# State-space products in rings of their own: what more temporary tiles do to a scheduled kernel

## The chip, the core and the metric

The kernel runs on one core of one Trainium2 chip. The metric is the device time of one execution in microseconds (us). On the core, TensorE (PE) multiplies matrices, VectorE (DVE), ScalarE (ACT) and GpSimd (POOL) work element by element, and SyncE (SP) issues the transfers of the DMA engines. Each engine takes its own instructions strictly in the order in which they stand in its queue. They wait for each other by semaphores.

## The reference

One layer of an encoder over 1024 positions of width 1024, all in float32:

```python
xn = rmsnorm(h, g_mix); proj = xn @ w_in
u, v = proj[..., :512], proj[..., 512:]
y_ssm = s5_mixer(u, ...)                    # 32 groups of 16 channels, 64 complex states, two directions
y_fft = fourier_mixer(v, w_fourier)         # 4 heads: real part of a 2-d FFT, then a 128x128 product
h = h + concatenate([y_ssm, y_fft]) @ w_out
h = h + conv_ffn(rmsnorm(h, g_ffn), w_up, conv_w, conv_b, w_down)   # 1024 -> 2x2816 -> 1024, width-3 convolution
return rmsnorm(h, g_final)

# s5_direction, run once per direction
lam_bar = exp(lam * dt)
b_bar = ((lam_bar - 1.0) / lam)[..., None] * b
bu = einsum('gph,blgh->blgp', b_bar, uf)
_, states = associative_scan(_ssm_combine, (a, bu), reverse=reverse, axis=1)
return einsum('ghp,blgp->blgh', c, states).real
# s5_mixer: y = both directions + d_skip * uf;  z = gelu(y);  z * sigmoid(z @ w_glu + b_glu)
```

## The kernel before

The sequence is cut into 128 chunks of 8 positions. Within a chunk the state-space part is a product with small matrices, and only the state at the chunk borders runs through a scan. The 32 groups are worked in 16 batches of two groups, b = 0 to 15. Four batches share a column tile `ct` of 128 channels, so batches 12 to 15 belong to tile 3. For each batch the program writes these steps, each a function:

- `prep(b)` (P): input factors. For the real and the imaginary part a product `b` of 128x512 (L666) and a sum of its halves into `bt` (L667). PE transposes `bt` (`pbm`) and multiplies it for the Toeplitz kernel (`pk`, L130). After every fourth batch `toeplitz` follows, with some DMAs through `dd`, `kd` and `tm`.
- `tables(b)` (T): twiddle tables `wt`. Two products `w` of 128x256 (L710), two sums (L712), two copies on ACT (L714).
- `out_matrix(b)` (OM): output factors `cm`. Two products `c` of 128x512 (L721), a sum (L723) and a difference (L725).
- `inputs(b)` (I): the matmuls `ps`, inputs to the states.
- `states(b)` (S): two products `r` of 128x512 from the incoming states in PSUM and `wt` (L745), sums into `scd` (L747, L749), four scans into `so` (L756, L757), two products `x` of 128x512 from the outgoing states and `wt` (L763), and two sums into `yy` (L764).
- `outputs(b)` (O): the matmuls `py` with `tm`, `yy` and `cm`, and after every fourth batch `gelu_out`: transposes `pyt` and a Gelu into `z`. `zsplit(ct)` splits `z` into high and low parts in `zf`.

Around these stand the products with `w_in` (`pin`), the Fourier part of four heads (splits `fw` and `yf`, evictions `yfs`, matmuls `pq`, `pe`, `po`), and the lower half of `w_out` (tokens WL and WB): `w_out_load(n)` loads and splits the four blocks k of column half n (`wo`, L155, one split each on DVE or POOL), and `w_out_bottom(n, s)` makes the 12 matmuls `pwo` of token tile s. DVE adds each result to `h` (L931). Behind the state-space part follow the gate products `pg` (weights `wg`, input `zf`), the upper half of `w_out`, a norm, the up projection as seven block products (`u`) with the convolution and gate, the down projection (`dqa`, `dqb`), and the final norm.

A float32 product of full precision is made of three matmuls of split operands, high and low.

Two things set the order of the work. The order in which the program is written is a string of tokens for this part, `SEQ`, and a table `OPT` says for each product and sum whether DVE or POOL does it. The change touches neither. The order in which instructions stand in each engine's queue is then set by the framework's scheduler, which plans with costs of its own and knows which tile each instruction writes. A tile comes from a ring: `bufs` tiles of one tag, handed out in turn. An instruction that takes a ring's next tile cannot run until the last reader of that tile's earlier content has run, so the size of a ring decides both waits and the plan.

Before, the rings of this part are: `t2`, two tiles of 2 KB per partition, shared by the products `b`, `r` and `x`; and `t3`, one tile, shared by `w`, `c` and the temporary `tw` of `phase_tables` (L511), where POOL makes the phase tables.

Of the kernel before, what the change touches and what calls it, by code (L numbers as in the profile page):

```python
# [20 lines left out]
P = 128  # L21
# [60 lines left out]
def bc(ap, axis, n):  # L82
    ap = ap.unsqueeze(axis)
    shape = list(ap.shape)
    shape[axis] = n
    return ap.broadcast_to(shape)
# [3 lines left out]
def encoder_block(  # L90
# [8 lines left out]
    V, A, PE, GP = nc.vector, nc.scalar, nc.tensor, nc.gpsimd  # L99
# [9 lines left out]
    def opt(key, default):  # L109
        v = OPT.get(key, default)  # L110
        return {"V": V, "G": GP}.get(v, v) if isinstance(v, str) else v
# [137 lines left out]
    def q(name, shape=(P, G), dt=F32, tag="q", bufs=13):  # L249
        return sp.tile(list(shape), dt, name=name, tag=tag, bufs=bufs)  # L250
# [4 lines left out]
    NG = 2  # L255
    NB = G // NG
# [77 lines left out]
    pwr, pwi, ta, tb = (pw[:, i] for i in range(4))  # L334
# [5 lines left out]
    def pair(a):  # L340
        return a.rearrange("p (b g) -> p b g", g=NG)
# [40 lines left out]
    def cmul(eng, outr, outi, ar, ai, br_, bi_, ta, tb):  # L382

        eng.tensor_mul(ta, ar, br_)
        eng.tensor_mul(tb, ai, bi_)
        eng.tensor_sub(outr, ta, tb)
        eng.tensor_mul(ta, ar, bi_)
        eng.tensor_mul(tb, ai, br_)
        eng.tensor_add(outi, ta, tb)

    def csq(c, s_, name):

        a, b, c2, s2 = (q(f"{name}_{k}") for k in "abcs")
        V.tensor_sub(a, c, s_)
        V.tensor_add(b, c, s_)
        V.scalar_tensor_tensor(s2, c, 2.0, s_, ALU.mult, ALU.mult)
        V.tensor_mul(c2, a, b)
        return c2, s2
# [96 lines left out]
    def phase_tables(lv):  # L495
        wt_ = w1t if lv == 4 else w2t
        te = opt(f"ph{lv}", GP)
        if lv == 4:
            ec, es, ecn = (prv[k] for k in ("ec", "es", "ecn"))
            esd = q("esd")  # L500
            V.tensor_copy(esd[0:64], es[0:64])
            V.tensor_copy(esd[64:128], ecn[64:128])
            prv["cur"] = (ec, esd)
        cur = prv["cur"]
        wr, wi = wt_[:, :, 0], wt_[:, :, 1]
        if lv == 2:
            GP.memset(wr[:, :, :, 0], 1.0)
            GP.memset(wi[:, :, :, 0], 0.0)
        for j in range(lv):
            n = 1 << j  # L510
            tw = q(f"tw{lv}_{j}", (P, 2, NB, NG, 8), tag="t3" if te is GP else "t2", bufs=1 if te is GP else 2)  # L511
            cmul(te, wr[:, :, :, n:2 * n], wi[:, :, :, n:2 * n], wr[:, :, :, :n], wi[:, :, :, :n],
                 bc(pair(cur[0]), 3, n), bc(pair(cur[1]), 3, n), tw[:, 0, :, :, :n], tw[:, 1, :, :, :n])
            cur = csq(cur[0], cur[1], f"wq{lv}_{j}")
        prv["cur"] = cur
        if lv == 2:
            GP.tensor_copy(w2t[:, :, 2], w2t[:, :, 0])
# [119 lines left out]
    def t2(name):  # L637
        return q(name, (P, 2 * NG * P), tag="t2", bufs=2)

    def prep_ct(ct):  # L640

        for dst, i in ((cbr, 0), (cbi, 1)):
            for d in range(2):
                hs = slice(64 * d, 64 * d + 64)
                A.activation(
                    dst[hs, :, d].rearrange("p (b g) h -> p b g h", g=NG),
                    rawc[hs, 4 * ct:4 * ct + 4, i], AF.Copy)
        cts[ct].kf = q(f"kf{ct}", (P, 8, 16), tag="kf", bufs=1)
        cts[ct].kb = q(f"kb{ct}", (P, 8, 16), tag="kb", bufs=1)
# [8 lines left out]
    def prep(b):  # L658

        c, ct, sb = bs[b], b // 4, b % 4  # L660
        if sb == 0:
            prep_ct(ct)
        bt = q(f"bt{b}", (P, 2, NG, 8, 16), tag="bt", bufs=1)
        for i, op in ((0, ALU.subtract), (1, ALU.add)):
            m = t2(f"b{b}_{i}").rearrange("p (n s h) -> p n s h", n=2 * NG, s=8)
            opt(f"pb{b}{i}", V).tensor_mul(m, slots(gst, b, i), heads(rawb, b))  # L666
            opt(f"pa{b}{i}", V).tensor_tensor(bt[:, i], m[:, 0:NG], m[:, NG:2 * NG], op)  # L667
        c.bm = q(f"bm{b}", (P, 2, NG, P), tag="bm", bufs=NBM)
        pt = bank2(f"pbm{b}")
        btv = bt.rearrange("p i g s h -> p (i g) (s h)")  # L670
        for n in range(2 * NG):
            PE.transpose(pt[:, n * P:(n + 1) * P], btv[:, n], ident)
        A.activation(c.bm.rearrange("p i g n -> p (i g n)"), pt, AF.Copy)
        pk = bank2(f"pk{b}")
        for g in range(NG):
            for i, cc in ((0, cbr), (1, cbi)):
                mm(pk[:, g * 32:(g + 1) * 32], btv[:, i * NG + g],
                   cc[:, NG * sb + g].rearrange("p d h -> p (d h)"), start=(i == 0), stop=(i == 1), key=f"pk{b}")
        pkv = pk[:, :NG * 32].rearrange("p (g d h) -> p g d h", g=NG, d=2)
        A.activation(cts[ct].kf[:, NG * sb:NG * sb + NG], pkv[:, :, 0], AF.Copy)  # L680
        A.activation(cts[ct].kb[:, NG * sb:NG * sb + NG], pkv[:, :, 1], AF.Copy)
        if sb == 3:
            toeplitz(ct)
# [20 lines left out]
    def tables(b):  # L704

        c = bs[b]
        c.wt = q(f"wt{b}", (P, 2, NG, 8, 16), tag="wt", bufs=2)
        for i, op in ((0, ALU.subtract), (1, ALU.add)):
            m = q(f"w{b}_{i}", (P, 2 * NG, 4, 16), tag="t3", bufs=1)
            opt(f"tw{b}{i}", GP).tensor_mul(m, bc(w1t[:, b].rearrange("p i g n -> p (i g) n"), 2, 4),  # L710
                                            bc(w2t[:, b, i:i + 2].rearrange("p i g n -> p (i g) n"), 3, 16))
            opt(f"ta{b}{i}", GP).tensor_tensor(c.wt[:, i, :, 4:8], m[:, 0:NG], m[:, NG:2 * NG], op)  # L712
            wf = c.wt[:, i].rearrange("p g j n -> p g (j n)")
            A.activation(wf[:, :, 0:64], wf[:, :, 127:63:-1], AF.Copy, scale=(-1.0 if i else 1.0))  # L714

    def out_matrix(b):
        c = bs[b]
        c.cm = q(f"cm{b}", (P, 2, NG, 8, 16), tag="cm", bufs=3)
        for i in range(2):
            m = q(f"c{b}_{i}", (P, 2 * NG, 8, 16), tag="t3", bufs=1)  # L720
            opt(f"tc{b}{i}", GP).tensor_mul(m, slots(pst, b, i), heads(rawc, b))  # L721
            if i == 0:
                opt(f"td{b}{i}", GP).tensor_add(c.cm[:, 0], m[:, 0:NG], m[:, NG:2 * NG])  # L723
            else:
                opt(f"td{b}{i}", GP).tensor_sub(c.cm[:, 1], m[:, NG:2 * NG], m[:, 0:NG])  # L725
# [10 lines left out]
    def states(b):  # L736

        c = bs[b]
        pst_ = c.ps
        A.activation(scr[:, :, 1:129], bc(r8[:, NG * b:NG * b + NG], 2, NCH), AF.Copy)  # L740
        sv = pst_.rearrange("p (i g c) -> p i g c", i=2, g=NG)
        wv = c.wt.rearrange("p i g j n -> p i g (j n)")
        for i in range(2):
            m = t2(f"r{b}_{i}").rearrange("p (i g c) -> p i g c", i=2, g=NG)
            V.tensor_mul(m, sv, wv if i == 0 else wv[:, ::-1])  # L745
            if i == 0:
                opt(f"ra{b}{i}", V).tensor_add(scd[:, 0, :, 1:129], m[:, 0], m[:, 1])  # L747
            else:
                opt(f"ra{b}{i}", V).tensor_sub(scd[:, 1, :, 1:129], m[:, 1], m[:, 0])  # L749
        n = 2 * NG * W  # L750
        so = q(f"so{b}", (P, 2 + n), tag="so", bufs=1)
        m = NG * W
        rf = scr.rearrange("p g w -> p (g w)")
        for i in range(2):
            df = scd[:, i].rearrange("p g w -> p (g w)")
            V.tensor_tensor_scan(so[0:64, 2 + i * m:2 + i * m + m], rf[0:64], df[0:64], 0.0, ALU.mult, ALU.add)  # L756
            V.tensor_tensor_scan(so[64:128, i * m:i * m + m][:, ::-1], rf[64:128, ::-1], df[64:128, ::-1], 0.0,  # L757
                                 ALU.mult, ALU.add)
        xs = so[:, 2:2 + n].rearrange("p (i g w) -> p i g w", i=2, g=NG)[:, :, :, :NCH]
        c.yy = q(f"yy{b}", (P, 2, NG, NCH), tag="yy", bufs=2)  # L760
        for i, op in ((0, ALU.subtract), (1, ALU.add)):
            m = t2(f"x{b}_{i}").rearrange("p (i g c) -> p i g c", i=2, g=NG)
            opt(f"xm{b}{i}", V).tensor_mul(m, xs, wv if i == 0 else wv[:, ::-1])  # L763
            opt(f"xa{b}{i}", V).tensor_tensor(c.yy[:, i], m[:, 0], m[:, 1], op)  # L764

# [627 lines left out]
    for i in range(2):  # L1393
        w = outer.tile([P, 2, 512], F32R, name=f"du{i}", tag="wp", bufs=NWP).bitcast(F32)
# [69 lines left out]
```

## Time and profile before

| | us |
|---|---|
| median of 3 runs | 1059.65 (1057.95 to 1060.36) |
| the profiled execution | 1058.18 |
| its span, first to last instruction | 1056.4 |
| PE busy in the span | 970.4 (92%) |
| DVE busy | 937.7 (89%) |
| ACT busy | 466.0 (44%) |
| POOL busy | 232.1 (22%) |

All times of the prediction come from the one profiled execution. Roughly, the span begins with norm and pole tables (to about 84 us), goes on with the state-space and Fourier parts (to about 306), the rest of the lower `w_out` and the gate (to about 359), the upper `w_out` and a norm (to about 440), the up projection (to 780) and the down projection with the final norm. Rows of stretches give for each engine the busy time and, in brackets, the number of instructions; then the share of TensorE's clock that was granted, the busy share of the DMA engines, and GB/s. Rows of waits read "engine, result, line, <- what released it: us in total, times, longest". Rows of a timeline read "start, duration, what"; in brackets the idle time just before and its releaser.

### The profile page before, as it was taken

To read this page: it belongs to the slowest core of one execution; us is meant where nothing else is said; L and a number is where in the kernel's file an instruction comes from. 1 tells how busy PE (TensorE), PEld (TensorE's weight loads), DVE (VectorE), ACT (ScalarE), POOL (GpSimd) and SP (SyncE) were. 2 spreads that over 40 slices of the span, in tenths; PEclk is the share of its full clock that TensorE was granted. 3 is DMA by queue.
4 is the path that set the end of the run, shared out by engine and by line. 5 is a ranking of instruction groups with operands and counts; after the bars stand their busy time and mean duration, and the time that the engine had idled before them with its cause. 6 is when DMAs were issued, how large, how long until landed. Compare 5 with 4: busy or idle time off the path is not lost.

```text
span 1056.4 us, 13491 instructions
## 1 busy us (share of the span) xinstructions
PE 970.4 (92%) x4504; PEld 798.5 (76%) x4504; DVE 937.7 (89%) x1721; ACT 466.0 (44%) x849; POOL 232.1 (22%) x243
## 2 busy tenths in 40 slices
PE   1799989758889999999999999999999999999995
PEld 1677767746767788788888888888887788888874
DVE  6988998999998889989988888889889588999977
ACT  4444232633122656544534445444454355545543
POOL 6257546775754003200000000000000000000400
PEclk9999898788999999999999999999999999999998
DMA  7242003242121323332322222322233399957554
GB/s 244 34 148 80 26 20 91 80 134 85 37 65 43 107 91 115 92 101 83 110 90 80 83 79 78 100 79 70 91 100 110 113 304 386 322 177 252 176 162 159
DMA packets 121596, 126.78 MB, mean 120 GB/s; under 512 B 17922, under 2 KB 86455, under 8 KB 121527
## 3 DMA queue, kind: packets, MB, share of 16 engines
q1 hardware_dynamic: 121382, 125.66, 37.3%
q8 instruction: 35, 0.57, 0.2%
q14 instruction: 35, 0.28, 0.1%
q10 hardware_dynamic: 144, 0.26, 0.1%
HBM read 103.35 MB, written 22.51 MB: 119 GB/s over the span
## 4 chain that ended last, share of the span: by engine, by line
PE 47%; DVE 8%; DMA 3%; issue 2%; ACT 1%; DVEq 0%; ACTq 0%
PE u L130 34%; PE dqa L130 7%; PE dqb L130 5%; DVE cg L1108 1%; DMA d_2a<-adr 1%; DMA wu<-in_w_up_dram 1%; DVE cv L1108 1%; DVE wo L155 0%; DMA d_4b<-in_w_down_dram 0%; DMA d_6b<-in_w_down_dram 0%; DVE ca L1248 0%; DVE n_t L196 0%; DVE hb L1322 0%; DVE cb L1248 0%; DMA d_8b<-in_w_down_dram 0%
## 5 line engine op out<-in xcount | busy, mean ns | idle before, releaser
L1330 POOL TENSOR_TENSOR hb<-hb,gl 128x512 f32<-128x512 f32 x8 | 13.0, 1655 | 548.2 <-ACT n_sq L1303 546.7
L130 PE MATMUL u<-xb,wo 128*128 128x512 f32 x528 | 129.9, 390 | 0.2 <-ACT xb L154 0.2
L130 PEld LDWEIGHTS u<-xb,wo 128*128 128x128 f32 x528 | 99.0, 188 | 21.8 <-ACT xb L154 0.6
L130 PE MATMUL u<-xa,wo 128*128 128x512 f32 x408 | 98.8, 390 | 0.5 <-DVE wo L155 0.4
L130 PEld LDWEIGHTS u<-xa,wo 128*128 128x128 f32 x408 | 76.4, 188 | 17.2 <-DVE wo L155 0.8
L154 ACT ACTIVATE wo<-wu 128x512 fp32r<-128x512 f32 x78 | 49.2, 630 | 85.4 <-PE u L130 58.1
L130 PE MATMUL pin<-xh,win 128*128 128x512 f32 x256 | 80.1, 414 | 1.4 <-ACT xh L227 1.4
L1108 DVE SCALAR_TENSOR_TENSOR cg<-ug,cw,cg 128x896 f32<-128x896 f32 (+1 forms) x88 | 62.2, 746 | 11.8 <-ACT cg L1103 11.8
L130 PE MATMUL u<-t4o,wo 128*128 128x512 f32 x264 | 63.4, 389 | 0.0
L1108 DVE SCALAR_TENSOR_TENSOR cv<-uv,cw,cv 128x896 f32<-128x896 f32 (+1 forms) x88 | 62.1, 745 | 0.0
L154 ACT ACTIVATE wo<-ws 128x512 fp32r<-128x512 f32 x32 | 20.2, 630 | 89.8 <-PE u L130 76.7
L130 PE MATMUL pwo<-wo,yf 128*128 128x512 f32 x192 | 52.1, 420 | 7.7 <-DVE h L931 2.8
L130 PEld LDWEIGHTS pin<-xh,win 128*128 128x128 f32 x256 | 50.1, 199 | 11.9 <-ACT xh L227 1.8
L130 PEld LDWEIGHTS u<-t4o,wo 128*128 128x128 f32 x264 | 49.6, 188 | 10.3
L155 DVE TENSOR_TENSOR wo<-wu,wo 128x512 fp32r<-128x512 f32 x78 | 54.5, 699 | 0.0
L130 PEld LDWEIGHTS pwo<-wo,yf 128*128 128x128 f32 x192 | 36.8, 200 | 17.0 <-DVE h L931 3.7
L130 PE MATMUL u<-t1o,wx 128*128 128x512 f32 x204 | 49.5, 389 | 0.0
L130 PE MATMUL u<-t2o,wx 128*128 128x512 f32 x204 | 49.5, 389 | 0.0
L130 PE MATMUL pin<-xl,win 128*128 128x512 f32 x128 | 47.2, 418 | 0.1
L130 PEld LDWEIGHTS u<-t1o,wx 128*128 128x128 f32 x204 | 38.3, 188 | 7.9
L130 PEld LDWEIGHTS u<-t2o,wx 128*128 128x128 f32 x204 | 38.3, 188 | 7.9
L714 ACT ACTIVATE wt<-wt 128x128 f32<-128x128 f32 x32 | 9.9, 308 | 65.0 <-POOL wt L712 41.5
(574 smaller groups left out, 2447.0 us busy)
## 6 DMA issues: line engine op xcount, KB each, us to landing
wu<-in_w_up_dram SPq DMA_DIRECT2D x88, 256.0 KB, 2.9
adr<-cg SPq DMA_DIRECT2D x22, 512.0 KB, 3.0
xr<-in_x_dram SPq DMA_DIRECT2D x8, 512.0 KB, 8.2
win_st<-in_w_in_dram SPq DMA_DIRECT2D x16, 256.0 KB, 2.9
wo_st<-in_w_out_dram SPq DMA_DIRECT2D x16, 256.0 KB, 3.0
h<-in_x_dram SPq DMA_DIRECT2D x8, 512.0 KB, 4.3
hdr<-h SPq DMA_DIRECT2D x8, 512.0 KB, 2.6
hb<-hdr SPq DMA_DIRECT2D x8, 512.0 KB, 4.5
```

The source lines that it names most:

```text
L130: i = PE.matmul(o, lhsT, rhs, start=start, stop=stop, skip_group_check=skip)
L154: A.activation(dst_hi, src, AF.Copy)
L155: return eng.tensor_sub(dst_lo, src, dst_hi.bitcast(F32))
L714: A.activation(wf[:, :, 0:64], wf[:, :, 127:63:-1], AF.Copy, scale=(-1.0 if i else 1.0))
L1108: i = V.scalar_tensor_tensor(cv[:, lo:hi], src[:, at:at + hi - lo], w, cv[:, lo:hi], ALU.mult, ALU.add)
L1330: GP.tensor_mul(hv(s, n), hv(s, n), gl[:, n * 512:(n + 1) * 512])
```

## The change

The input factors' products `b` get a ring `tb` of two tiles, the outgoing states' products `x` get a ring `tx` of two tiles, the incoming states' products `r` keep `t2` alone with its two tiles, and `t3` gets two tiles instead of one. Eight tiles instead of three, 10 KB more per partition.

```diff
@@ phase_tables
-            tw = q(f"tw{lv}_{j}", (P, 2, NB, NG, 8), tag="t3" if te is GP else "t2", bufs=1 if te is GP else 2)
+            tw = q(f"tw{lv}_{j}", (P, 2, NB, NG, 8), tag="t3" if te is GP else "t2", bufs=2 if te is GP else 2)
@@ prep
-            m = t2(f"b{b}_{i}").rearrange("p (n s h) -> p n s h", n=2 * NG, s=8)
+            m = q(f"b{b}_{i}", (P, 2 * NG * P), tag="tb", bufs=2).rearrange("p (n s h) -> p n s h", n=2 * NG, s=8)
@@ tables
-            m = q(f"w{b}_{i}", (P, 2 * NG, 4, 16), tag="t3", bufs=1)
+            m = q(f"w{b}_{i}", (P, 2 * NG, 4, 16), tag="t3", bufs=2)
@@ out_matrix
-            m = q(f"c{b}_{i}", (P, 2 * NG, 8, 16), tag="t3", bufs=1)
+            m = q(f"c{b}_{i}", (P, 2 * NG, 8, 16), tag="t3", bufs=2)
@@ states
-            m = t2(f"x{b}_{i}").rearrange("p (i g c) -> p i g c", i=2, g=NG)
+            m = q(f"x{b}_{i}", (P, 2 * NG * P), tag="tx", bufs=2).rearrange("p (i g c) -> p i g c", i=2, g=NG)
```

The instructions are the same; the scheduler sets another order. The first place where DVE's queue differs is early in the state-space part (a row is the line, the operation, result<-inputs and the shape; the number at a name's end tells tiles apart):

```order
 L155 TENSOR_TENSOR win_0_1506<-win_0_st,win_0_1506 128x512
+L725 TENSOR_TENSOR cm_859<-c_1_863 128x256
+L721 TENSOR_TENSOR c_0_881<-pst,rawc 128x512
 L667 TENSOR_TENSOR bt_838<-b_0_839 128x256
 L667 TENSOR_TENSOR bt_838<-b_1_842 128x256
 L666 TENSOR_TENSOR b_1_927<-gst,rawb 128x512
-L725 TENSOR_TENSOR cm_859<-c_1_863 128x256
-L721 TENSOR_TENSOR c_0_881<-pst,rawc 128x512
-L667 TENSOR_TENSOR bt_923<-b_0_924 128x256
-L667 TENSOR_TENSOR bt_923<-b_1_927 128x256
 L710 TENSOR_TENSOR w_0_888<-w1t,w2t 128x256
```

The difference that makes an output factor, and the next product behind it, moved ahead of a batch's input factors; the input factors of the next batch moved behind the table products.

The second place is DVE's queue around the splits of the second column half of the lower `w_out` (`wo_1_1` is block k=1). `r_0_2826` and `scd` there belong to batch 14, `w_0_2738` is batch 15's table, `so_2865` are the scans of batch 15, `yy_2785` is batch 13:

```order
 L931 TENSOR_TENSOR h_2712<-h_2712,pwo_3_3031 128x512
-L764 TENSOR_TENSOR yy_2785<-x_0_2786 128x256
+L756 SCALAR_TENSOR_TENSOR so_2865<-scr,scd 64x260
+L757 SCALAR_TENSOR_TENSOR so_2865<-scr,scd 64x260
 L155 TENSOR_TENSOR wo_1_1_2660<-wo_1_1_st,wo_1_1_2660 128x512
-L745 TENSOR_TENSOR r_0_2826<-ps_2673,wt_2714 128x512
 L155 TENSOR_TENSOR wo_1_2_2665<-wo_1_2_st,wo_1_2_2665 128x512
 L931 TENSOR_TENSOR h_2584<-h_2584,pwo_2_3045 128x512
 L155 TENSOR_TENSOR wo_1_3_2670<-wo_1_3_st,wo_1_3_2670 128x512
-L747 TENSOR_TENSOR scd<-r_0_2826 128x2x128
 L155 TENSOR_TENSOR wg_3154<-wg_st,wg_3154 128x512
-L745 TENSOR_TENSOR r_1_2829<-ps_2673,wt_2714 128x512
```

The states of batch 14 stood behind the split of `wo_1_1` and now stand ahead of it, all scans of batch 15 too: the split is DVE's instruction 606 before and 631 after.

The third place is PE's queue where the first column half of the lower `w_out` ends (`pwo_2_3045`) and the second goes on. `py_2944`, `py_2952` and `py_2974` are the outputs of batches 13, 14 and 15, and `pwo_5_2877` and `pwo_4_2995` are the first to read `wo_1_1`:

```order
+L130 MATMUL py_2974<-tm_2710,u_2214 128x128
 L130 MATMUL pwo_2_3045<-wo_0_0_2588,yf 128x512 x3
 L130 MATMUL pwo_2_3045<-wo_0_1_2593,yf 128x512 x3
 L130 MATMUL pwo_2_3045<-wo_0_2_2598,yf 128x512 x3
 L130 MATMUL pwo_2_3045<-wo_0_3_2603,yf 128x512 x3
+L130 MATMUL py_2944<-cm_2818,yy_2785 128x128
+L130 MATMUL py_2944<-tm_2710,u_2214 128x128
+L130 MATMUL py_2944<-cm_2818,yy_2785 128x128 x2
+L130 MATMUL py_2952<-cm_2937,yy_2837 128x128 x2
+L130 MATMUL py_2952<-tm_2710,u_2214 128x128
+L130 MATMUL pwo_5_2877<-wo_1_1_2660,yf 128x512
```

The outputs of batches 13 and 14, and a first product of batch 15, moved ahead of the products with `wo_1_1`; those of batch 12 did too, a little earlier in the queue.

## The prediction

> **What bounds the kernel now.** I read the stages first (busy time of each engine per stretch), then the chain of the work that ended last, then DVE's waits in the first long stretch, then the two timelines at the point where DVE hands over to PE. The stretches are cut at 85.8 us (first place where the order of DVE differs), 305.9 and 307.5 (the hand-over), 358.6 (end of the gate products `pg`), 440.6 and 780.
>
> ```profile
> core 0: us, PE busy (x) PEld busy (x) DVE busy (x) ACT busy (x) POOL busy (x), PEclk, DMA share, GB/s
> 85.80:305.90 220.10, 182.07 (x980) 152.43 (x979) 203.38 (x323) 68.71 (x186) 146.16 (x164) 0.87 0.21 64
> 307.50:334.80 27.30, 25.77 (x132) 21.16 (x133) 27.08 (x41) 4.81 (x12) 13.59 (x13) 1.00 0.13 40
> 334.80:358.60 23.80, 23.18 (x106) 18.96 (x105) 16.07 (x25) 14.35 (x24) 1.29 (x1) 1.00 0.30 100
> 358.60:440.60 82.00, 79.98 (x380) 65.24 (x378) 76.33 (x163) 49.66 (x103) 16.04 (x11) 1.00 0.31 103
> 440.60:780.00 339.40, 339.35 (x1496) 280.90 (x1497) 303.55 (x463) 151.50 (x208) 0.00 (x0) 1.00 0.29 88
> 780.00:1056.40 276.40, 263.97 (x1153) 215.15 (x1152) 239.53 (x426) 134.64 (x237) 12.99 (x8) 0.99 0.62 211
> ```
>
> In the first row DVE is busy 203.38 of 220.10 us and PE only 182.07: the state-space stretch belongs to DVE. From 307.5 on PE has the work that fills the time (25.77 of 27.30, 23.18 of 23.80, 79.98 of 82.0, 339.35 of 339.4), so a start that comes earlier or later at 307.5 is carried to the end almost unchanged. The chain of the last-ended work agrees:
>
> ```profile
> 440.65 339.56 PE u L130 x1496
> ```
>
> It is one unbroken run of PE; it and the row before it cannot give back what the state-space stretch loses. What DVE waits for in that stretch:
>
> ```profile
> DVE cm L725 <- POOL c L721: 2.9, 2, 1.8
> DVE bt L667 <- PE pk L130: 2.2, 1, 2.2
> DVE w L710 <- POOL cm L725: 1.8, 1, 1.8
> DVE yfs L888 <- ACT yfs L885: 1.6, 1, 1.6
> DVE r L745 <- POOL yy L764: 1.3, 2, 0.6
> DVE w L710 <- POOL wt L712: 1.1, 1, 1.1
> ...
> DVE b L666 <- POOL yy L764: 0.6, 1, 0.6
> ```
>
> DVE's idle time is 220.10 - 203.38 = 16.7 us. The waits that the shared rings can be behind are those on `c`, on the table tiles and on `yy` (which frees an `x`): 2.9 + 1.8 + 1.3 + 1.1 + 0.6 = 7.7. The other 9.0 are transposes, Fourier evictions and the like, which no edited line touches.
>
> The hand-over, PE's timeline and then DVE's:
>
> ```profile
> 298.91 4.60 PE L130 MATMUL pwo<-wo,yf 128*128 128x512 f32 x12 [2.32 <-DVE h L931]
> ...
> 307.52 4.14 PE L130 MATMUL pwo<-wo,yf 128*128 128x512 f32 x17 [1.01 <-DVE wo L155]
> ```
>
> ```profile
> 305.87 1.59 DVE L155 TENSOR_TENSOR wo<-wo_st,wo 128x512 fp32r<-128x512 f32 x1
> ```
>
> PE stands still until DVE has split block k=1 of the second half of `w_out`'s lower part (`wo1_1_1`); after that it is nowhere held for more than a few tenths. So the forecast is the time of this split in the new order, and the PE work behind it.
>
> **The change, part by part.** No arithmetic is added or removed: the same products on the same engines, in tiles of the same size. A matter of rings alone has two effects: waits for a free tile go, and the scheduler, which knows the rings, sets other orders.
>
> *Waits that go.* At best all 7.7 us. Three of them are at the very start:
>
> ```profile
> 91.33 1.32 DVE L725 TENSOR_TENSOR cm<-c 128x256 f32<-128x256 f32 x1 [1.82 <-POOL c L721]
> ...
> 97.35 1.31 DVE L710 TENSOR_TENSOR w<-w1t,w2t 128x256 f32<-128x256 f32 x1 [1.82 <-POOL cm L725]
> ...
> 101.19 0.43 DVE L710 TENSOR_TENSOR w<-w1t,w2t 128x256 f32<-128x256 f32 x1 [1.05 <-POOL wt L712]
> ```
>
> The wait before `cm` is for a POOL product, not for a tile, and in the new order this `cm` stands two `bt` rows earlier, so DVE meets the same POOL product sooner. The two on `w` are ring waits in the true sense and may go. POOL's own waits for ring tiles (the first row below is not one of them, the second is) are off the path, POOL being busy 146 of 220 us:
>
> ```profile
> POOL yy L764 <- DVE x L763: 16.7, 8, 4.5
> ...
> POOL c L721 <- DVE cm L723: 6.7, 5, 3.1
> ```
>
> *Work put ahead.* The new order runs the state-space batches ahead of the Fourier part and of `w_out`. On DVE the split `wo1_1_1` moves from place 606 to 631 of its instructions: 25 instructions are put ahead of it and none is left behind. All belong to batches 13 to 15 and to the split of `z2`, and before they stood just behind it, in the row 307.50:334.80. At that row's mean, 27.08 / 41 = 0.66 us, they take 25 x 0.66 = 16.5 us. They ran there beside a PE that was busy; now PE waits for them, because DVE works its queue in order.
>
> *The same work on PE.* PE may do less behind the hand-over, since 19 of 24 small `py` matmuls of the last four batches now stand ahead of it. One batch is six of them:
>
> ```profile
> 295.09 0.38 PE L130 MATMUL py<-tm,u 128*128 128x128 f32 x2
> ...
> 295.98 0.61 PE L130 MATMUL py<-cm,yy 128*128 128x128 f32 x4
> ```
>
> From 295.09 to 296.59 is 1.5 us, 0.25 for each of the six, so 19 are worth 4.7 us. PE's busy time from the hand-over to the end of `pg` is 25.77 + 23.18 = 48.95; less 4.7, and with the 0.6 us of idle that the second row has (the 1.5 us in the first I let go, as DVE is 16.5 us freer there): 44.8 us. Bounds: 48.95 - 4.7 = 44.2 without any idle, and 51.1 - 4.7 = 46.4 with all of it.
>
> *The sum.* Let X be DVE's idle time from 85.8 to the split. The split ends at 85.8 + 203.4 + 16.5 + 1.6 + X = 307.3 + X, and `pg` at 307.3 + X + 44.8 = 352.1 + X, against 358.6 now. The shift is X - 6.5. Without idle from rings X is 9.0 (shift +2.5); with the idle of before, 16.7 (+10.2). I take 12: the 9.0 that is not a matter of rings, and of the 7.7 the 2.9 on `c`, which is a wait for a product. That gives 9.0 + 2.9 = 11.9, a shift of +5.4 us.
>
> *A second path.* PE reaches the hand-over itself only after the first half of this `w_out`, whose start hangs on the last Fourier rows:
>
> ```profile
> 263.43 0.73 PE L130 MATMUL pwo<-wo,yf 128*128 128x512 f32 x2 [2.20 <-ACT yf L154]
> ...
> 291.35 3.90 PE L130 MATMUL pwo<-wo,yf 128*128 128x512 f32 x16
> ```
>
> Ahead of those rows DVE has 28 instructions more, 25.1 us by their own entries in the trace. Behind them PE has 97 `pwo` matmuls at 3.90 / 16 = 0.244 (23.7 us), 29 `py` at 0.25 (7.2 us) and 8 transposes (1.0 us). How DVE's idle time lies around this point (us, DVE busy):
>
> ```profile
> 85.80:264.90 179.10, 165.48 (x272) 0.86 0.23 70
> ```
>
> With 13.6 us of DVE's 16.7 lying ahead of it, PE arrives at 263.4 + 25.1 - 13.6 + 31.9 = 306.8 plus the idle of DVE up to there, plus its own waits. Before, it came 1 us early; now it is nearly level with DVE, so a fall of DVE's idle time in the last 40 us gains nothing, and more than some 3 us of PE's own waits there is paid. For that I add 1 us: a shift of +6.4.
>
> *Products beside POOL.* The 16.5 us may stretch. DVE's products with both inputs in SBUF take longer in this stretch than those that read PSUM:
>
> ```profile
> L666 DVE TENSOR_TENSOR b<-gst,rawb 128x512 f32<-128x512 f32 x21 | 22.9, 1112 | 0.8 <-POOL yy L764 0.6
> L745 DVE TENSOR_TENSOR r<-ps,wt 128x512 f32<-128x512 f32 x28 | 18.3, 679 | 1.4 <-POOL yy L764 1.3
> L763 DVE TENSOR_TENSOR x<-so,wt 128x512 f32<-128x512 f32 x21 | 18.0, 887 | 0.3
> ```
>
> Same size, 1112 and 887 ns against 679. POOL also has to do more ahead of the hand-over: of its 13.59 us in 307.50:334.80 nearly 11 (the entries of the ten products and sums concerned) now come before. The Trainium skill, page "SBUF — State Buffer", section "Who interferes with whom", says that a DVE instruction with two SBUF inputs shares a read interface with GpSimd, under an exclusive lock, while one with a single SBUF input does not; the three rows agree (`r` reads PSUM for one input). By a full lock, as that page has it, each of those 11 us would be lost to DVE, and the sum would be +17. In the rows the loss over 220 us is smaller: `b` 21 x 0.43 and `x` 21 x 0.21 lose 13.4 us beside 146 us of POOL, 0.09 of it, or 1 us of 11 for these two; with other two-input products perhaps 0.3, 3 us, of which the durations taken from 307.50:334.80 hold most, since POOL worked there too. I take 0 and keep 0 to +11 for the range.
>
> *The rest.* Some `wo_st`, `wg_st`, `h` and `kd` loads change places on SP's queue: DMA is busy 0.21 and 0.13 there, I take 0 and bound it by 1 us to either side. In the last stretch, at the end of `dqa`, a few rows change places; ±1.5 us.
>
> The profiled execution took 1058.18 us (span 1056.4), 1.5 below the median of the runs, 1059.65. By it the forecast is 1058.2 + 6.4 = 1064.6, against the median 1066. I say 1065.
>
> **Rivals.** One: the wait on POOL dissolves nearly wholly and the kernel is faster. Its place is DVE's idle time before 305.9, and it decides below X = 6.5. With X = 2 the shift is -4.5: 1054 to 1055; with X = 0, 1052 to 1053. For it: DVE never waits long for any one thing (2.2 us at most), and batches that start earlier leave slack everywhere. Against it: 9.0 of the 16.7 us name no ring, and the path through PE holds it up from below.
>
> Two: the change does not move the time. X near 6.5, or a gain in durations (shorter `b` and `x`, if POOL meets them less often) that pays for the 25 instructions: within 0.2% of 1059.65, that is 2.1 us, about what a measurement of this kernel can tell from no change. That the change does nothing at all is excluded by the orders; that the delay is hidden would need slack behind 307.5, of which the rows leave 1.5 + 0.6 + 2.0.
>
> Three: worse than forecast. DVE is as idle as before (+10.2), or POOL is late with `c` of batch 14 and `yy` of batch 14, which now stand ahead of the hand-over on PE's queue too; with the stretching beside POOL, +10 to +17: 1069 to 1076. For it: POOL goes one work after another through DVE (16.7 us in eight waits for `x`) and does more before the hand-over. Against: it has 74 us of idle time.
>
> **How the numbers follow.** Forecast, slower by 2 to 10 us: 0.42. Three: 0.16. Two: 0.19. One: 0.23. Slower by over 0.2% is forecast and three, 0.58; same 0.19; faster 0.23. The range leaves out the better half of the first rival and the last part of the third, 1055 to 1075; the forecast alone spans 1062 to 1070.
>
> **What would show it.** In the changed kernel's trace PE should wait for DVE's second `wo` split with `pwo` until about 319 (now 307.5), with batches 13 to 15 of DVE before it; `pg` should end near 364 to 365; the stretch from there to the end should be as long as now. DVE's waits named `w` <- POOL should be gone, `cm` <- POOL `c` should still be there. I am wrong if DVE's idle time falls below 7 us, if the wait that PE ends on is another one, if the mean of `b` and `x` moves by more than a tenth of a us, or if the stretch behind 358.6 changes its length.

## The result and the profile after

The changed kernel takes 1072.29 us, median of 4 runs (1071.13 to 1074.45), beside 1058.9 (1057.95 to 1060.36) for the kernel before: a ratio of 1.0132 with a 95% interval of 1.0118 to 1.0147, or 13.4 us slower. In a second session, shown below, the ratio is 1.0105. The forecast was 1065.0. The profiled execution took 1072.66, its span is 1070.9, 14.5 more than before.

The stretches of the kernel after, cut at the same events as those of before (the columns are: from:to, us, then busy us and instructions of each engine, granted clock, DMA share, GB/s). 323.1 is the end of the split of `wo1_1_1`, 367.0 the end of `pg`:

```profile
core 0: us, PE busy (x) PEld busy (x) DVE busy (x) ACT busy (x) POOL busy (x), PEclk, DMA share, GB/s
85.80:323.10 237.30, 182.71 (x1016) 154.80 (x1015) 225.57 (x351) 73.16 (x196) 160.00 (x174) 0.88 0.19 59
323.10:367.00 43.90, 43.90 (x204) 36.57 (x203) 28.21 (x44) 17.67 (x30) 4.00 (x3) 1.00 0.25 79
...
449.00:789.00 340.00, 339.67 (x1498) 281.00 (x1498) 304.08 (x464) 151.72 (x210) 0.00 (x0) 1.00 0.29 89
824.10:1070.90 246.80, 232.72 (x1005) 189.65 (x1003) 209.32 (x378) 113.83 (x208) 13.23 (x8) 0.97 0.64 221
```

and the first and the last of them in the kernel before, where the same events lie at 307.5 and 814.7 (the first `dqa`):

```profile
85.80:307.50 221.70, 182.68 (x981) 152.59 (x979) 204.98 (x324) 70.31 (x190) 147.76 (x165) 0.87 0.21 63
814.70:1056.40 241.70, 229.75 (x1005) 187.48 (x1003) 208.98 (x378) 114.60 (x208) 12.99 (x8) 0.99 0.66 225
```

The split ends 15.6 us later, `pg` 8.4 us later (367.0 against 358.6), the first `dqa` 9.4 us later (824.1 against 814.7), the span 14.5. So 8.4 us are lost up to the gate, 1.0 between it and the down projection, and 5.1 behind that (246.8 against 241.7). Between, PE is full, as it was (339.67 of 340.0).

PE at the hand-over of the kernel after (start, duration, what, in brackets the idle time ahead and its releaser), then DVE there:

```profile
316.11 4.61 PE L130 MATMUL pwo<-wo,yf 128*128 128x512 f32 x12 [2.90 <-DVE h L931]
...
322.72 6.19 PE L130 MATMUL pwo<-wo,yf 128*128 128x512 f32 x26
```

```profile
321.72 0.70 DVE L757 TENSOR_TENSOR_SCAN so<-scr,scd 64x260 f32<-64x260 f32 x1
322.45 2.29 DVE L155 TENSOR_TENSOR wo<-wo_st,wo 128x512 fp32r<-128x512 f32 x2
```

Scans of batch 15, the last in the first row, stand directly ahead of the splits, as the order said. PE has its last stop at 316.1, of 2.90 us, for an addition to `h`, and then runs without a gap to the end of `pg`: the second row of stretches is full, 43.90 of 43.90. By the order of its queue, the one `pwo` at 322.0 (in the part left out) is its first product with `wo1_1_1`, 1.1 us ahead of the end of the split; no wait for the split shows. So PE and the split are level there, and the wait on which PE ends is for another row of DVE.

What DVE waits for from 85.8 to 330 in the kernel after, the four largest (us in total, times, longest):

```profile
DVE cm L725 <- POOL c L721: 2.3, 2, 2.1
DVE w L710 <- POOL wt L712: 2.3, 2, 1.6
DVE bt L667 <- PE pk L130: 2.0, 2, 1.7
DVE cb L839 <- POOL vv L834: 1.3, 2, 1.0
```

### The profile page after: what moved, and what is told of

Same layout as the page of the kernel before. It is cut to its first block, busy times and chain, and to the rows that moved or that the text cites. A ratio compares the mean times of both kernels' runs of the same rounds, so it can differ in the third digit from the quotient of the medians.

```text
span 1070.9 us, 13482 instructions
## 1 busy us (share of the span) xinstructions
PE 969.0 (90%) x4504; PEld 799.2 (75%) x4504; DVE 942.6 (88%) x1721; ACT 465.6 (43%) x849; POOL 235.6 (22%) x243
## 4 chain that ended last, share of the span: by engine, by line
PE 44%; DVE 8%; DMA 5%; issue 2%; ACT 1%; SPq 0%; DVEq 0%; ACTq 0%
PE u L130 34%; PE dqa L130 7%; PE dqb L130 3%; DMA bb<-in_w_down_dram 1%; DVE cg L1108 1%; DMA cb<-in_w_down_dram 1%; DMA wu<-in_w_up_dram 1%; DMA d_6a<-adr 0%; DVE wo L155 0%; DVE cv L1108 0%; DMA d_3b<-in_w_down_dram 0%; DVE n_t L196 0%; DMA first_st<-in_w_down_dram 0%; DMA d_9b<-in_w_down_dram 0%; DMA d_7b<-in_w_down_dram 0%
## 5 line engine op out<-in xcount | busy, mean ns | idle before, releaser
L130 PE MATMUL pin<-xh,win 128*128 128x512 f32 x256 | 79.8, 412 | 12.2 <-ACT vt L619 11.1
L130 PEld LDWEIGHTS u<-xa,wo 128*128 128x128 f32 x408 | 76.3, 188 | 17.4 <-ACT ug L1124 1.1
L130 PE MATMUL pwo<-wo,yf 128*128 128x512 f32 x192 | 49.7, 414 | 8.3 <-DVE h L931 4.5
L221 PE MATMUL n_pt<-ident,xr 128*128 128x128 f32 x64 | 12.7, 350 | 27.1 <-DVE xr L292 10.2
```

The lines of the kernel that those rows point to most:

```text
L130: i = PE.matmul(o, lhsT, rhs, start=start, stop=stop, skip_group_check=skip)
L221: PE.transpose(pt[:, k * P:(k + 1) * P], xk, ident)
```

## The experiments

Sizes of rings and the order of the queues changed together. To part them, an order was written into the changed kernel: at the end of `encoder_block` each queue (DVE, ACT, POOL, PE, SP) is given its sequence of instructions by edges between neighbours. They are marked as needing no synchronization, so they set the order of issue alone. The only thing that differs from kernel to kernel is the table `ORDERS`.

```diff
+    chain_orders(tc, nc)
+def chain_orders(tc, nc):
+    orders = json.loads(zlib.decompress(base64.b85decode(ORDERS)))
+    by = {i.name: i for i in nc.cur_bb.bb.instructions}
+    for seq in orders.values():
+        for a, b in zip(seq, seq[1:]):
+            tc.add_manual_dep(by[f"I-{b}"], f"I-{a}", mybir.DependencyInfo(
+                mybir.DependencyClass.NoSync, mybir.DependencyReason.DATA), reason="issue order")
```

In what follows "hand-over" is the end of the split of `wo1_1_1`, and the times of marks are from the profiled execution of each kernel. Ratios are to the kernel before, run on the same chip in turn.

### The rings alone, in the order of before

The changed kernel with `ORDERS` from the kernel before.

> The changed kernel's rings, with every engine's queue held in the order of the kernel before by issue-order edges. Theory A, the order carries the loss: the time of the kernel before, 1059 us, or up to 3 us less where waits for a free tile go; DVE's split of block wo1_1_1 again near 306 to 307, the end of pg near 358. Rival B, the rings themselves cost (more POOL work beside DVE's two-input products, the 4 us by which DVE's busy time before the split exceeded the sum): 1063 to 1068. Rival C, the rings alone gain much and the order took it away: 1052 or less.

Measured: 1054.81 us (1052.85 to 1056.59, 11 runs) against 1057.47, ratio 0.9967 (0.9956 to 0.9977). The rings by themselves are a gain. The stretch up to the hand-over of this kernel, and DVE's waits in it:

```profile
85.80:304.40 218.60, 181.19 (x980) 152.04 (x978) 208.20 (x326) 70.04 (x190) 148.87 (x164) 0.88 0.21 64
```

```profile
DVE bt L667 <- PE pk L130: 1.9, 1, 1.9
DVE yfs L888 <- PE pe L130: 1.8, 1, 1.8
```

DVE's idle time falls from 16.7 us (221.70 - 204.98) to 10.4, and the wait on POOL's `c`, 2.9 us before, is no longer among the longest, which these two now lead. But its busy time rises by 3.2 us. Of these, 1.1 are two rows that ran just ahead of 85.8 before, as the counts 326 and 324 say; the rest is in rows that became longer. The net is 3.1 us, and the span is 3.1 us shorter (1053.3).

### Where the new order costs: head or tail

The changed kernel, first with the order of before up to the middle of the up projection and the new order behind it, then the reverse.

> The changed kernel's rings; queues in the order of the kernel before up to the middle of the up projection, in the changed kernel's order behind it (the down projection). Theory A, the changed kernel loses 8.8 us ahead of the down projection and 5.7 us in it, each by its own order: 1059 + 5.7 = 1064 to 1065. Rival, the loss in the down projection is no matter of order but of its later start or of chance: 1059.

> The changed kernel's rings; queues in the changed kernel's order up to the middle of the up projection, in the order of the kernel before behind it. Theory A: 1059 + 8.8 = 1067 to 1068, the stretch of the down projection 276.4 us again. Rival (the loss there follows the late start, or the clock): 1072, as the changed kernel.

Measured: old head and new tail, 1055.76 us (1054.25 to 1057.88, 12 runs), ratio 0.998 (0.9971 to 0.9989); new head and old tail, 1069.55 (1068.17 to 1069.93, 5 runs), 1.0107 (1.0091 to 1.0123). The loss is in the head. The first lies below both of its expected times, which had no gain of the rings in them; the second lies between its two. The last stretch, from the first `dqa` on, in the kernel with the new tail alone, and in the changed kernel profiled a second time:

```profile
810.50:1053.30 242.80, 230.08 (x1005) 187.50 (x1003) 209.47 (x378) 114.05 (x208) 13.73 (x8) 0.99 0.65 224
```

```profile
825.50:1070.80 245.30, 231.41 (x1005) 188.68 (x1003) 209.50 (x378) 114.49 (x208) 13.22 (x8) 0.98 0.64 222
```

The tail's own order costs 1.1 us here (242.8 against 241.7), and 1.7 and 1.8 in two kernels further down that have it too (243.4 and 243.5), not the 5.1 of the profile after. Where the others come from is told below.

### The 25 rows alone

The kernel of the first experiment (rings, order of before), with one block moved: the 25 DVE instructions of batches 13 to 15 and of `z2` ahead of the split, the `py` of batches 12 to 14 on PE ahead of the `pwo` that read it, and with them four rows on ACT's queue and five on POOL's. A few rows of DVE's order:

```diff
 L764 TENSOR_TENSOR yy_2785<-x_0_2786 128x256
-L155 TENSOR_TENSOR wo_1_1_2660<-wo_1_1_st,wo_1_1_2660 128x512
+L710 TENSOR_TENSOR w_0_2738<-w1t,w2t 128x256
 L745 TENSOR_TENSOR r_0_2826<-ps_2673,wt_2714 128x512
-L155 TENSOR_TENSOR wo_1_2_2665<-wo_1_2_st,wo_1_2_2665 128x512
...
```

> The changed kernel's rings and the order of the kernel before, as in the first experiment (1054.8), with one block of the new order alone: the 25 DVE rows of batches 13 to 15 and of z2 go ahead of the split of wo1_1_1, and the py matmuls of batches 12 to 14 ahead of the pwo that read it (ACT's and POOL's rows that these need go with them). The Fourier part and the first half of w_out stay where they were. Theory A, the 25 rows ahead of the hand-over are the cost (16.5 us by the sum, some 4 us more if DVE's products stretch beside POOL, less 7 us of PE work that is done earlier): the split near 321 to 324 (304.4 in the first experiment), pg ends near 366 to 369, 1065 to 1068. Rival, the late Fourier part and first half of w_out carry the loss: 1055 to 1060.

Measured: 1065.96 us (1064.13 to 1066.88, 5 runs) against 1057.85, ratio 1.0072 (1.0058 to 1.0085). Against the rings alone (0.9967) that is 0.0105 of 1058, 11.1 us.

```profile
85.80:321.80 236.00, 184.27 (x1014) 155.02 (x1013) 225.29 (x351) 72.02 (x195) 160.04 (x174) 0.89 0.19 59
304.00:322.00 18.00, 8.77 (x38) 8.09 (x39) 17.86 (x26) 3.65 (x9) 11.06 (x12) 0.63 0.00 0
322.00:366.50 44.50, 44.09 (x203) 36.36 (x203) 27.00 (x40) 16.86 (x29) 3.77 (x3) 1.00 0.23 78
```

PE's longest stop ahead of the hand-over:

```profile
316.90 0.79 PE L130 MATMUL py<-cm,yy 128*128 128x128 f32 x2 [8.01 <-DVE cm L725]
```

In the 18 us ahead of the hand-over DVE is full (17.86) and PE stands half of the time (8.77); then PE is full for 44.5 us. The split comes 17.4 us later than with the rings alone (321.8 against 304.4), `pg` 11.0 later (366.6 against 355.6). DVE's busy time up to the split is 17.1 us larger (225.29 - 208.20). The marks are as the first theory had them, and its bound of 1065 to 1068 held. But PE does not stand at the split: it stands for 8.0 us at a `py` that was put ahead too, for the output factor `cm`, one of the 25 rows, and reaches `pwo` at 321.2 without a wait for the split. The rows on DVE and the `py` on PE moved together, so what each does alone is not shown.

### One ring at a time, in the order that the scheduler gives it

Three kernels: only `tb` for the products `b`; only `tx` for the products `x`; only `t3` with two tiles.

```diff
# first
+            m = q(f"b{b}_{i}", (P, 2 * NG * P), tag="tb", bufs=2).rearrange("p (n s h) -> p n s h", n=2 * NG, s=8)
# second
+            m = q(f"x{b}_{i}", (P, 2 * NG * P), tag="tx", bufs=2).rearrange("p (i g c) -> p i g c", i=2, g=NG)
# third (and the same for c and tw)
+            m = q(f"w{b}_{i}", (P, 2 * NG, 4, 16), tag="t3", bufs=2)
```

> The kernel before with one part of the change alone: the input factors' products b in a ring of their own, in the order that the scheduler then makes. By DVE's queue, 2.5 us of work (net, in the durations of before) are put ahead of the split of wo1_1_1 and 8.2 us ahead of the last Fourier split yf. Theory A, split and Fourier both count, less 2 us of waits that go: 1058 to 1062. Rival, rings alone: 1055 to 1057.

> The kernel before with only the outgoing states' products x in a ring of their own. By DVE's queue the split of wo1_1_1 has 1.7 us less ahead of it and the last yf 3.7 us less. Theory A: 1055 to 1058. Rival, any new order of the scheduler costs: above 1060.

> The kernel before with only the ring of output factors and tables at two tiles. By DVE's queue the split of wo1_1_1 has 3.0 us less ahead of it, the last yf the same. Of the ring waits 5.8 us (on c and w) are this ring's. Theory A: 1052 to 1057. Rival, any new order of the scheduler costs: above 1060.

Measured against 1057.26: `tb` 1058.49 us (1055.2 to 1062.4, 12 runs), ratio 1.001 (0.9999 to 1.0021); `tx` 1062.16 (1060.94 to 1063.7, 5 runs), 1.0045 (1.0033 to 1.0057); `t3` 1063.49 (1059.56 to 1066.25, 6 runs), 1.0058 (1.0041 to 1.0075). The first came as expected; the other two did not, and lie where their rival had them, above 1060. No single ring makes the loss of all three, and none of them makes a gain: each gets another order. Both misses have the hand-over earlier than before, at 303.7 and 303.3, and still lose. From there to the end of `pg`, `tx`:

```profile
303.70:362.10 58.40, 53.61 (x256) 43.67 (x255) 48.15 (x70) 22.79 (x43) 19.71 (x20) 0.97 0.19 59
```

with these stops of PE in it:

```profile
329.42 0.49 PE L130 MATMUL py<-cm,yy 128*128 128x128 f32 x2 [1.49 <-DVE cm L725]
...
346.12 1.21 PE L130 MATMUL pg<-zf,wg 128*128 128x512 f32 x4 [1.83 <-ACT zf L154]
```

and `t3`, with PE's waits:

```profile
303.30:359.20 55.90, 49.54 (x245) 40.79 (x246) 46.03 (x70) 20.50 (x38) 15.32 (x14) 1.00 0.19 65
```

```profile
PE py L130 <- DVE yy L764: 3.2, 2, 1.8
PE py L130 <- DVE cm L725: 2.2, 1, 2.2
```

PE takes 58.4 and 55.9 us for the stretch that took 51.1 before. In it PE now waits for the rest of the state-space part: for `cm` and `yy` of the last batches with `py`, in `tx` also for `zf` with `pg`. It is idle for 4.8 us in `tx` and 6.4 in `t3`, where it was 2.15 before (51.1 - 48.95). In `t3` that is nearly all of the loss in this stretch. In `tx` the larger part, 4.7 us, is more busy time: PE has 256 matmuls there instead of 238, and the granted clock is 0.97. So two things hang on DVE's queue at this place, the splits for `w_out` and the last batches for the gate, and the rows suggest that one pays for the other; that it is the whole loss is not shown. (The profiled execution of `t3` was its fastest, 1059.56, so its rows show a part of that loss.)

### The hand-over still earlier

If the splits are late, one would put them first. Two tries: the changed kernel with the additions to `h` and the splits moved up and `py` and `pyt` moved down; and the kernel of the first experiment with the additions and splits moved up 3 to 7 places and `py` of batches 14 and 15 behind a part of `pg`. From the second, a few rows of DVE's order:

```diff
 L721 TENSOR_TENSOR c_0_2729<-pst,rawc 128x512
+L155 TENSOR_TENSOR wo_1_1_2660<-wo_1_1_st,wo_1_1_2660 128x512
 L756 SCALAR_TENSOR_TENSOR so_2780<-scr,scd 64x260
 L757 SCALAR_TENSOR_TENSOR so_2780<-scr,scd 64x260
...
 L764 TENSOR_TENSOR yy_2785<-x_0_2786 128x256
-L155 TENSOR_TENSOR wo_1_1_2660<-wo_1_1_st,wo_1_1_2660 128x512
```

> The changed kernel with its own order, but DVE's adds of pwo to h for token tiles 6, 3 and 2 and the splits of wo1_1_1 to wo1_1_3 put ahead of rows of batches 13 to 15 (3 to 14 places up), and PE's py of batches 13 to 15 and the last transposes put behind pwo matmuls that need none of them. Theory A, in the changed kernel the hand-over waits for DVE's place in the queue, above all for the add that frees the PSUM bank (PE idle 2.9 us ahead of pwo_0_2 at 316.1): PE runs on from about 309, pg ends 5 to 7 us earlier, 1065 to 1067. Rival, DVE's whole work up to the last state-space batch is the bound: the wait only moves to py15 and the z3 transposes, gain under 2 us, 1070 to 1072.

> The changed kernel's rings and the order of the kernel before, as in the first experiment (1054.8), but around the hand-over DVE's adds of token tiles 6 and 3 and the splits of wo1_1_1 and wo1_1_2 go 3 to 7 places up, ACT's copies for these splits ahead of one scr copy, and PE's py of batches 14 and 15 behind two pg matmul groups. Theory A2, both ends of DVE's queue count, the adds and splits that PE waits for and the state-space rest behind them: PE loses its waits of 2.1, 1.7 and 1.0 us before the hand-over and pg ends 2 to 4 us earlier: 1051 to 1053. Rival, the state-space rest (z3) binds: 1054 to 1056.

Measured: the first 1072.46 us (1072.23 to 1075.63, 4 runs), ratio 1.0144 (1.0126 to 1.0162), no gain on the changed kernel; the second 1056.91 (1054.66 to 1060.1, 12 runs), 0.9987 (0.9973 to 1.0), no better than the rings alone. The split came earlier in both, at 318.1 (instead of 323.1) and at 298.5 (instead of 304.4). PE in the first, ahead of `pg`:

```profile
344.56 0.96 PE L130 MATMUL pg<-zf,wg 128*128 128x512 f32 x3 [1.44 <-DVE h L931]
```

Behind this wait and one of 1.37 us, also for an addition to `h`, the granted clock is 0.50 from 345.8 to 352.7, which cost about 3 us, half of the 5.8 us in which PE is busy there: a part of the answer to why the earlier split gave nothing.

PE in the second:

```profile
335.69 1.09 PE L788 MATMUL pyt<-ident,ys 128*128 128x128 f32 x8 [0.47 <-ACT ys L778]
...
346.24 4.14 PE L130 MATMUL pg<-zf,wg 128*128 128x512 f32 x10 [1.97 <-ACT sg L990]
```

and in the kernel with the rings alone, for comparison:

```profile
335.94 1.04 PE L788 MATMUL pyt<-ident,ys 128*128 128x128 f32 x8
```

The split came 5.9 us earlier in the second, the last transposes only 0.25 (335.69 against 335.94). That fits the rival's reading, that the rest of the state-space part sets `pg`, but does not show it: in this order a part of `pg` stands ahead of the last `py`, and of PE's waits between 325 and 337 (0.80 for `wg`, 0.47 for `ys`) none is for a row of DVE's state-space part.

### A wait of 11 us that the prediction did not see

In the kernel after PE stands still once for long, in the middle of the head. Its row, and ACT's rows there:

```profile
169.84 0.79 PE L130 MATMUL pin<-xh,win 128*128 128x512 f32 x1 [11.09 <-ACT vt L619]
```

```profile
165.02 0.42 ACT L740 ACTIVATE scr<-r 128x256 f32<-128x256 f32 x1 [9.83 <-DVE so L757]
...
169.19 2.06 ACT L619 ACTIVATE vt<-pin 128x512 f32<-128x512 f32 x4
```

The evictions `vt`, which free the PSUM banks for `pin`, stand in ACT's new order behind a copy `scr` that waits 9.83 us for a scan on DVE. The experiment is the changed kernel with the evictions, and the first `z` of tile 0, ahead of that copy, run beside the changed kernel once more. (An order with these rows ahead of two such copies ends in a deadlock, where each waits for the other, and has no time.)

```diff
+L619 ACTIVATE vt_1661<-pin_0_1611 128x512
+L619 ACTIVATE vt_1661<-pin_1_1612 128x512
 L740 ACTIVATE scr<-r_97 128x2x128
 L714 ACTIVATE wt_1368<-wt_1368 128x2x64 x2
```

> The changed kernel in its own order, but on ACT's queue the first z of tile 0 and the evictions vt of two w_in results are put ahead of a copy scr that waits for DVE's scans, and of two wt copies that wait for POOL. In the changed kernel PE stood still for 11.1 us there, waiting for such a vt. Theory A, DVE's queue sets the end of the state-space stretch and PE has slack there: PE's wait shrinks to 1 to 3 us, the time stays within 2 us of the changed kernel's, 1070 to 1074. Rival, PE's lost 11 us are what the change costs: 1062 to 1066.

> The changed kernel once more, for its last stretch: in the profile the granted clock fell to 0.5 there for some 6 us behind two short waits of PE, worth 2.9 us, and in the kernel before it didn't. If that is a matter of where the waits fall in time and not of this kernel's order, this profile may show it or not, and the time moves with it between 1068 and 1073. If the order brings it: again about 1072, with the lowered clock at the same place.

Measured: 1068.34 us (1067.13 to 1071.76, 6 runs), ratio 1.01 (1.0082 to 1.0118); the changed kernel in the same session 1069.9 (1067.77 to 1072.59, 5 runs), 1.0105 (1.0087 to 1.0122). The two can't be told apart, and their intervals leave at most some 4 us between them: the 11 us are slack, or most of them. PE waits elsewhere instead, by this row of its waits:

```profile
PE pbm L672 <- POOL bt L667: 8.4, 1, 8.4
```

Where DVE's queue sets the end of a stretch, the length of one wait on PE says little.

## Why the prediction was right or wrong, step by step

**The mechanism was right in the queue, and wrong in the row that PE waits for.** Most of the loss is the block of 25 instructions ahead of the split, paid in full on DVE and in part given back behind it. Alone it costs 17.4 us at the split where the prediction had 16.5, and 11.0 us at the end of `pg`; what the prediction gave back by `py` done earlier (4.7 us and a little idle time) is the difference of 6.4. But PE was to stand at the second `wo` split until about 319. Its last wait in the kernel after is for an addition to `h`, until 316.1, and with the block alone for a `cm`; in neither does it wait for the split. That is one of the prediction's own signs of being wrong, "if the wait that PE ends on is another one". All three rows stand in the same queue of DVE, within some 7 us ahead of the split's end, so the sum by the split still gives the end of `pg`: 323.1 + 43.9 = 367.0. A second sign holds too: the stretch behind `pg` grew by 6.1 us (703.9 against 697.8). The reading that PE is held behind 307.5 "nowhere for more than a few tenths" was not exact either: POOL's `cm` held it 1.0 us in the kernel before.

**DVE's idle time X** was forecast at 11.9 and measured at 11.7 (237.30 - 225.57). The total is right, its parts are not all: the ring waits `w` <- POOL should be gone, and 2.3 us of them remain, while `cm` <- POOL `c` is 2.3 instead of 2.9 and drops out of the list when the rings are alone. It was called a wait for a product; with the rings alone, in the order of before, it is gone, so the old rings held that product back; the new order brings a wait of 2.3 us for it again. That the total fits is in part luck.

**The work behind the hand-over** was forecast at 44.8 us and measured at 43.9. The second path, PE's own queue, is the one on which PE's last wait lies, level with the split as the prediction feared; the sum by the split needed no 1 us for it.

**First term that was mis-sized: products beside POOL.** It was taken as 0 within 0 to +11; DVE's busy time up to the split came to 225.57 where the sum had 221.5 (203.4 + 16.5 + 1.6), so it is +4.1. The groups of DVE in that stretch of the kernel after (instructions | busy us, mean ns | idle), to be held against the three rows of the prediction:

```profile
L666 DVE TENSOR_TENSOR b<-gst,rawb 128x512 f32<-128x512 f32 x22 | 23.0, 1063 | 0.1
L763 DVE TENSOR_TENSOR x<-so,wt 128x512 f32<-128x512 f32 x22 | 21.0, 978 | 0.1
L745 DVE TENSOR_TENSOR r<-ps,wt 128x512 f32<-128x512 f32 x32 | 20.8, 681 | 0.5 <-ACT wt L714 0.4
```

`x`, with both inputs in SBUF, went from 887 to 978 ns (22 x 0.09 = 2.0 us), `b` from 1112 to 1063 (-1.1 us), and `r`, which reads PSUM, stayed (679 and 681). The rest is spread over other rows: of the larger groups, the scans of L756 went from 848 to 906 ns and `yy` from 672 to 778, while `bt` fell from 767 to 662. The Trainium skill, page "SBUF — State Buffer", section "Who interferes with whom", has just this division: with two SBUF inputs a DVE product shares a read interface with GpSimd, with one it does not. That agrees; its full lock, which by the prediction would have cost 11 us here, does not show. By the experiments the 4.1 us are for the most part not the new order's: with the rings alone DVE's busy time rises by 3.2 already, 1.1 of it by two rows that ran ahead of 85.8 before, and the 25 rows take 17.1 instead of 16.5. A DVE that waits less runs more of its rows beside POOL; that this is the cause of the other 2.1 us of the 3.2 was not tested by itself.

**Second term that was mis-sized: the last stretch.** Taken as 0 within 1.5 us, it was +5.1 in the profiled execution. PE's waits there in the kernel after, then in the kernel before:

```profile
PE dqa L130 <- DVE d_8bo L1205: 1.4, 1, 1.4
PE dqb L130 <- DVE dp L1346: 1.3, 1, 1.3
PE dqa L130 <- DVE d_7bo L1205: 1.2, 1, 1.2
PE dqb L130 <- ACT d_2bo L1204: 0.7, 1, 0.7
```

```profile
PE dqa L130 <- DVE d_8bo L1205: 1.4, 1, 1.4
PE dqa L130 <- DVE d_7bo L1205: 1.0, 1, 1.0
```

The two new ones, 1.3 and 0.7, come from rows that changed places: `dp` additions stand behind splits of `d` now. The larger part is not a wait. The granted clock fell behind the waits for `d_7bo` and `d_8bo`, in the kernel after (first fence, three rows) and not in the kernel before at the same matmuls (second fence). The cuts are at the places where the granted clock can change, as told in the last section:

```profile
1040.25:1043.67 3.42, 1.63 (x6) 1.00 0.01 2
1043.67:1047.08 3.41, 2.52 (x6) 0.50 0.00 0
1047.08:1050.49 3.41, 3.41 (x9) 0.50 0.57 226
```

```profile
1027.01:1030.42 3.41, 2.38 (x12) 1.00 0.00 0
1030.42:1033.83 3.41, 1.97 (x7) 1.00 0.01 2
```

(Of the engines only PE is given.) Half of 2.52 + 3.41 us of work, about 3.0, was lost by it. In the changed kernel run again it took one such stretch, with 2.94 us of work, about 1.5; that is the whole difference of its last stretch (245.3 against 246.8). In the three others with the same tail order the clock did not fall. So this part hangs on the moment at which the waits come, more than on the order: the kernel before waits 2.5 us here (1.02 + 1.44), nearly as long as the kernel after (2.7), but over two of these stretches, where after nearly all of it falls into one. As both profiles of the changed kernel show it, a share of its order is not excluded. In medians the changed kernel and the one with the old tail differ by 0.0025 of the time at most (1.0132 against 1.0107; 1.0105 in the other session), 0 to 2.6 us.

**A term that the sum didn't have.** The 25 rows with the rings stand at 1.0072, the whole new head with the old tail at 1.0107: some 3.7 us are in the rest of the head's order. Marks of the two kernels show 2.0 of them ahead of the split (323.8 against 321.8) and 1.0 between the end of `pg` and the first `dqa` (456.9 against 455.9 us). Which rows they are was not taken apart.

So the forecast's +6.4 became +14.5 in the profiled execution by +4.1 of DVE's busy time, +1.0 between `pg` and the down projection (taken as 0 within 1 for the DMAs; its cause was not looked for), +5.1 in the last stretch, 3.0 of it by the moment at which the clock fell, and about -2 in what the sum had too large (0.9 behind the hand-over, 0.2 of X, the 1 for the second path). 10.2 us in one direction came from three places that had been costed at zero.

**The rivals.** The first, faster by waits that dissolve, is what the rings do by themselves: X is 10.4 there, above its bound of 6.5, but with the 25 rows left where they were there is nothing to pay. It priced the gain with the loss in the same sum and so could not see it. The third, worse by 10 to 17 us, gave the time, and its range holds it, though by none of the ways it named alone: X was not that of before (11.7, not 16.7), the stretching was 4.1 us at most, and DVE waited no longer for POOL's `c` (2.3 us, 2.9 before). That it holds the time owes something to chance, as the last stretch adds 5.1 us that it did not have. That a split could come earlier without a gain, as in four of the experiments, no case said: the sum took the split as the only thing that binds, where in two of them PE then waits for rows of the last batches.

## What to carry to other kernels

Where a scheduler sets the order, a larger ring is two changes: fewer waits, here 0.33% faster, and another order, here some 1.4 to 1.7% slower than the rings alone; hold the order of before by edges of issue and time the rings apart, which also gave the best kernel of the study (1054.81 us against 1057.47). At a point where one in-order queue feeds two consumers, count for both what stands ahead: instructions moved ahead of a hand-over cost their whole duration there, less only what the waiting engine is thereby spared behind it, and instructions moved the other way can make the second consumer late. A term costed at zero because its rows "only change places" should carry a range to the loss side of a few waits of the size that the stretch already shows.

## What the runs showed of the hardware

Two short waits of PE, 1.23 and 1.45 us, three matmuls apart, were followed by 6.8 us at half the clock. Single rows of PE there and at the same place before:

```profile
1044.56 1.22 PE L130 MATMUL dqa<-d_8bo,d_8ao 128*128 128x512 f32 x2 [1.45 <-DVE d_8bo L1205]
...
1047.29 1.48 PE L130 MATMUL dqa<-d_6bo,d_6ao 128*128 128x512 f32 x3
```

```profile
1032.80 0.73 PE L130 MATMUL dqa<-d_8bo,d_8ao 128*128 128x512 f32 x2 [1.44 <-DVE d_8bo L1205]
...
1034.29 0.84 PE L130 MATMUL dqa<-d_6bo,d_6ao 128*128 128x512 f32 x3
```

The same three matmuls took 1.48 us against 0.84.

The traces' records of the granted clock say when this happens. In all thirteen profiled executions (the two kernels, the changed one again, and ten of the experiments) they know two values, 1.00 and 0.50. In each trace the 0.50 comes in stretches that begin on one grid of 3.413 us and last one to five times that (114 stretches, 3.41 to 17.07 us). The grid does not begin with the program: it lies elsewhere in each execution. Ahead of each drop PE had been busy at most 2.15 us in the grid's last 3.41; and between 84 and 1045 us no stretch of the grid at the full clock in which PE was busy less than 1.5 us was followed by another at the full clock. Between 1.5 and 2.15 both occur. At the waits for `d_7bo` and `d_8bo` PE was busy 1.63 and 1.25 us of one stretch in the two executions where the clock fell, and 1.94 or more in each stretch in the eleven others. So the same waits cost nothing or 3 us, by how they fall on the grid.

The Trainium skill, page "TensorE: Matmul & The Clock Gate", section "Part 1: The HAM clock gate (the "warmup" mystery)", says that the clock gate watches a free-running window of about 3.4 us and goes to half the clock after an idle one. The grid of 3.413 us, its place that changes from execution to execution, and the half clock agree with that. That the window must be idle does not: 1.63 us of work in 3.41 did not keep the clock up.
